# Conditioning dots moved beside wider units, one engine per portion of u, and a new order for the first norm in a streaming-encoder block

## The chip, the core and the metric

The kernel runs on one core of a Trainium2 chip. The core has a matrix engine (TensorE, in the profile PE for matmuls and PEld for the loads of their stationary operand), three engines for elementwise work (VectorE = DVE, ScalarE = ACT, GpSimd = POOL), and a queue that issues most DMAs (SyncE = SP). Each engine works through its own instructions in program order and waits for others by semaphores. The metric is the device time of one execution in microseconds (us), lower is better. The time of the kernel before is 1076.0 us, the median of three runs.

## The reference

One block works on a sequence of 512 frames with 1024 channels. All parameters are float32. With `D = 1024`, `F = 2816`:

```python
mod = (silu(c) @ w_ada + b_ada).reshape(B, 3, 3, D)      # 9 vectors of 1024 values
h = rms_norm(x, g_ffn1) * (1 + mod[:, 0, 1]) + mod[:, 0, 0]
x = x + 0.5 * mod[:, 0, 2] * swiglu(h, w_ffn1_in, w_ffn1_out)

h = rms_norm(x, g_mix) * (1 + mod[:, 1, 1]) + mod[:, 1, 0]
u_pool, u_ssm, gl_pool, gl_ssm = split(h @ w_in)         # 512, 512, 1024, 1024 channels
y_pool = multiscale_pool(u_pool, ...) @ w_pool_up
y_ssm = s5_mixer(u_ssm, ...) @ w_ssm_up                  # complex diagonal scan over time, GELU, GLU
merged = sigmoid(gl_pool) * y_pool + sigmoid(gl_ssm) * y_ssm
x = x + mod[:, 1, 2] * (merged @ w_out)

h = rms_norm(x, g_ffn2) * (1 + mod[:, 2, 1]) + mod[:, 2, 0]
x = x + 0.5 * mod[:, 2, 2] * swiglu(h, w_ffn2_in, w_ffn2_out)
return rms_norm(x, g_final)
```

`rms_norm` divides by the root of the mean of squares over the 1024 channels; `swiglu` is `(silu(h @ A) * (h @ B)) @ w_out`, with `A` and `B` of 2816 columns each. The conditioning vector `c` needs a product with a matrix of 1024 x 9216 (`w_ada`).

## The kernel before

**Layout.** Channels lie on the 128 partitions and time runs along the free dimension: `X` holds the residual stream as 8 tiles of 128 channels by 512 frames. Each float32 product is made of three matmuls of reduced-precision halves (`mm3`, lines 258 to 261): a tile of weights or activations is split into a rounded part (`hi`, made by ScalarE) and a rest (`lo`, made by VectorE), and `hi*hi`, `hi*lo` and `lo*hi` are added up in one PSUM bank.

**Units.** The program is a list of units (class `Unit`, line 46). A unit has a source of weights in HBM, a number of weight columns (at most 1024 by 128 rows), a function `mm` that issues matmuls, and optional functions `pre` and `post` around it. A unit of 1024 columns in the first feed-forward part has 24 matmuls of 512 columns, one of 640 has 15, one of 768 has 18. Units without weights (`pe_unit`) hold other work of the mixer. The loop at the end (line 1370) goes through them: `pre`, then `prefetch` (which splits the weights of a unit two ahead, and issues the DMA of one further ahead, by a plan worked out in lines 1262 to 1286), then `mm`, then `post`, then the side work of that index. Raw weights have three buffers, split ones three. The order within every engine is the program's order; nothing is rescheduled.

**Parts.** (1) The start: `c` is loaded, `silu` applied and broadcast to all partitions by two matmuls into `C`; `X` is loaded tile by tile; squares of `X` are made by ScalarE and added up by VectorE in two sums (`ACC` and `odd`, `sq_acc`, line 179); four matmuls with a column of ones turn the sum into one value for each frame (`norm_sum`); ScalarE takes the root, VectorE the reciprocal `rc`, and `norm_rows` spreads it over the partitions by matmuls with the identity `IDN`. `keep_warm` issues dummy matmuls on TensorE, as many as `WARM` tells at four places. (2) Eight units of `group6` make the first seven column groups of the feed-forward part while `h` of block `k` is being made (`make_h1`: VectorE's product `X * GS * r` at line 218 and ScalarE's rounded copy; `make_h2`: VectorE's rest at line 249). (3) The rest of the first feed-forward part goes in blocks of hidden tiles (`BLOCKS`): for every block first the units of 1024 columns that make gated hidden tiles, then eight units that multiply them by the second matrix, of 128 columns for each hidden tile of the block. (4) The mixer, (5) the second feed-forward part, where pairs of hidden tiles are made by seven products in place of eight (`ffn_seven`): each pair has units of 1024 and 768 columns, and the second ones come a step later than the first. (6) The last norm.

**Conditioning.** Each of the 72 columns of `mod` is a dot of a 128 x 1024 tile of `w_ada` with `C`, one VectorE instruction (`ada_dot`, line 132) after a DMA of 512 KB. Sixteen are made in the first eight units (shift and scale of the first norm), eight beside units 10 to 17 (the first gate), and the other 48 one by one by `ada_step`, from unit 16 on, after every unit, with two buffers: a dot, then the DMA of the next tile into the buffer just freed.

**Small work.** From unit 18 on a list `fill` gives each unit of the first feed-forward part some work on the S5 parameters: ten small VectorE operations each (`some(SMALL)`), then tables made by GpSimd (`ssm_table`), then four batches of GpSimd, TensorE and VectorE work.

**The mixer's front.** `post6` takes the first results out of PSUM. `ssm_u(m, p)` copies portion `m` of the S5 input (one PSUM bank) into `U` in sixteen pieces of 32 x 128, which reorders time and channels; `pool_in` and `pool_fin` make the pooling groups; `ssm_in`, `ssm_scan` and `ssm_out` the scan, on VectorE above all. In between stand units of gate matmuls (`gp`) that keep TensorE at work.

Of the kernel before, what the change touches and what calls it, by code (L numbers as in the profile page):

```python
# [10 lines left out]
F32 = mybir.dt.float32  # L11
F32R = mybir.dt.float32r
I32 = mybir.dt.int32
AF = mybir.ActivationFunctionType
ALU = mybir.AluOpType

P = 128
T = 512
KT = 8
NF = 22  # L20
BLOCKS = ((0, 5), (5, 10), (10, 16), (16, 22))
NPAIR = 16
WINDOWS = (2, 4, 8, 16)
EPS = 1e-6
SA = 2
LA = 4
SMALL = 10
WARM = (6, 14, 2, 6)
MAGIC = 12582912.0


# [23 lines left out]
def block_kernel(ctx, tc, a, out):  # L55
    nc = tc.nc
# [48 lines left out]
    def ev(dt=F32):  # L105
        return evp.tile([P, T], dt, tag="ev", name="ev")
# [72 lines left out]
    def sq_acc(k, eng, cs=ALL, odd=None):  # L179
        acc = odd if odd is not None and k % 2 else ACC  # L180
        if k == 0 or odd is not None and k == 1:
            S.activation(out=acc[:, cs], in_=X[:, k, cs], func=AF.Square)
        else:
            sq = ev()
            S.activation(out=sq[:, cs], in_=X[:, k, cs], func=AF.Square)  # L185
            eng.tensor_tensor(out=acc[:, cs], in0=acc[:, cs], in1=sq[:, cs], op=ALU.add)  # L186
# [4 lines left out]

    def norm_sum(pc, cs=ALL, more=()):

        b0, b1 = cs.start // P, cs.stop // P
        terms = [ACC] + list(more)
        for n, x in enumerate(terms):
            for b in range(b0, b1):
                E.matmul(pc[:, b:b + 1], x[:, b * P:(b + 1) * P], ONE[:, 0:1], start=n == 0 and b == b0,
                         stop=n == len(terms) - 1, skip_group_check=True)
        sd = smp.tile([P, 4], F32, tag="sd", name="sd")  # L200
        S.activation(out=sd[:, b0:b1], in_=pc[:, b0:b1], func=AF.Sqrt, bias=EPSC, scale=1.0 / 1024.0)
        rc = smp.tile([P, 4], F32, tag="rc", name="rc")
        V.reciprocal(out=rc[:, b0:b1], in_=sd[:, b0:b1])
        return rc
# [10 lines left out]
    def make_h1(s, k, part):  # L215
        r, cs = part
        t = ev()
        V.scalar_tensor_tensor(  # L218
            out=t[:, cs], in0=X[:, k, cs], scalar=GS[:, s * 8 + k:s * 8 + k + 1], in1=r[:, cs],
            op0=ALU.mult, op1=ALU.mult,  # L220
        )
        S.activation(out=HH[:, k, cs], in_=t[:, cs], func=AF.Identity, bias=shift_col(s, k))  # L222
        if s == 2:
            S.activation(out=HF[k % 4][:, cs], in_=t[:, cs], func=AF.Identity, bias=shift_col(s, k))
            made[k] = made.get(k, 0) + cs.stop - cs.start
        return t
# [222 lines left out]
    def ffn_seven(s, w6, win, wout, wend):  # L449
# [175 lines left out]
        def out_units(f0, f1, ds=range(KT), lastb=False):  # L625
            units.extend([out_unit([d], f0, f1, wout[d, :, f0 * P:f1 * P], [], lastb=lastb) for d in ds])
# [10 lines left out]
        for i in range(18):  # L637
            units.extend(seq[i][0])
            if i:
                units.extend(seq[i - 1][1])  # L640
            if i in (6, 12):
                out_units(i - 2, i + 4)
        units.extend(seq[17][1])
        hold = []
        units.append(out_unit(range(2), 16, 20, wend[:, 0:1024], hold, True, False))
# [77 lines left out]
    def tt_(o, x, y, op):  # L723
        vq.tensor_tensor(out=o, in0=x, in1=y, op=op)
# [272 lines left out]
    def ssm_u(m, p):  # L997
        for b in range(4):
            for t in range(4):
                o, i = U[0][32 * t:32 * t + 32, 4 * m + b, :], p[32 * b:32 * b + 32, t * P:(t + 1) * P]  # L1000
                if t % 2:
                    V.tensor_copy(out=o, in_=i)  # L1002
                else:
                    S.copy(out=o, in_=i)
# [108 lines left out]
    def mixer():  # L1113
# [95 lines left out]
        units.extend([u_unit(0), pf[3], u_unit(1), pf[2], si[0], gp[0], pf[0], sc[0], gp[1], pf[1], si[1], gp[2], sc[1], gp[3], pw_unit()])  # L1209
        units.extend([si[2], gp[4], sc[2], up[0], gp[5], si[3], up[1], sc[3], gp[6], up[2], so[0], gp[7], up[3]])  # L1210
        units.extend([so[1], gs[0], so[2], so[3]])
        units.extend(gs[1:7])
        units.extend([glu_unit(j) for j in range(4)])
        units.append(gs[7])
# [11 lines left out]
    def ada_first(n):  # L1226
        if spots:
            t = spots.pop(0)
            nc.sync.dma_start(out=t, in_=a["w_ada"][n])
            ada_tiles[n] = t  # L1230
        else:
            ada_load(n)

    def h_and_dots(k):
        t = make_h1(0, k, r0)
        if k < KT - 1:
            ada_dot(8 + k + 1)
            make_gs(0, k + 1, k + 2)
        make_h2(0, k, t, r0)
        if k < KT - 1:  # L1240
            ada_dot(k + 1)

    def pre0(k):
        if k < 3:
            ada_pair(k + 5)
        if k == 0:
            h_and_dots(0)
        if k < KT - 1:
            h_and_dots(k + 1)

    ffn(0, a["w_f1_6"], a["w_f1_in"], a["w_f1_out"], pre0)
    n_ffn1 = len(units)
    mixer()
    ffn_seven(2, a["w_f2_6"], a["w_f2_in"], a["w_f2_out"], a["w_f2_end"])

    raws, ws, due = {}, {}, []
# [7 lines left out]
    for j, u in enumerate(wu):  # L1264
        if u.kind == 2:
            t = wu.index(u.twin)
            split_at[j] = seconds[-4] + 1 if len(seconds) >= 4 else t - 1
            load_at[t] = load_at.get(t)
            seconds.append(j)
            continue  # L1270
        split_at[j] = max(walls[-3] + 1, j - 4) if len(walls) >= 3 else 0
        if j < KT:
            split_at[j] = j - 1
        walls.append(j)
        if u.kind == 1:
            jobs.append(j)
        else:
            back = split_at[raws_of[-3]] if len(raws_of) >= 3 else -9
            load_at[j] = max(split_at[j] - (3 if seconds else 2), back) if j > 3 else -1
            raws_of.append(j)  # L1280
# [7 lines left out]
    def load(j):  # L1288
        if j < len(wunits):
            u = units[wunits[j]]  # L1290
            if u.load:
                u.load()
                return
            t = rawp.tile([P, 1024], F32, tag="raw", name="raw")
            nc.sync.dma_start(out=t[:, 0:u.cols], in_=u.src)
            raws[j] = t

    def split(j):
        if j < len(wunits):
            u = units[wunits[j]]  # L1300
            if u.split:
                ws[j] = u.split()
                return
            t = raws.pop(j)[:, 0:u.cols]
            hi = wp.tile([P, 1024], F32R, tag="wh", name="wh")
            lo = wp.tile([P, 1024], F32R, tag="wl", name="wl")
            S.copy(out=hi[:, 0:u.cols], in_=t)  # L1307
            eng = G if u.pool_lo else V
            eng.tensor_tensor(out=lo[:, 0:u.cols], in0=t, in1=hi[:, 0:u.cols].bitcast(F32), op=ALU.subtract)  # L1309
            ws[j] = (hi, lo)  # L1310

    def prefetch():
        while due:
# [6 lines left out]
    def ada_pair(k):  # L1320
        ada_first(8 + k)
        ada_first(k)

    nc.sync.dma_start(out=C0, in_=a["c"].unsqueeze(0))
    for k in range(KT):
        nc.sync.dma_start(out=X[:, k, :], in_=a["x"][:, k, :])
    nc.sync.dma_start(out=COL[:, 0:120], in_=a["cols"])
    ada_first(8)
    load(0)
    ada_first(0)  # L1330
    nc.sync.dma_start(out=IDN, in_=a["ident"])
    for k in (1, 2):
        load(k)
        ada_pair(k)
# [4 lines left out]
    def keep_warm(n):  # L1339

        for _ in range(n):
            E.matmul(warm[:, 0:P], ONE, ONE, start=True, stop=True)
# [4 lines left out]
    pcs = [ps(), ps()]  # L1347
    for h in range(2):
        E.matmul(pcs[h], ONE[0:1, :], C0[:, h * T:(h + 1) * T], start=True, stop=True)
    odd = ev()  # L1350
    for d in range(KT):
        sq_acc(d, V, odd=odd)
    for h in range(2):
        S.copy(out=C[:, h * T:(h + 1) * T], in_=pcs[h])
    tt_(ACC, ACC, odd, AD)
    keep_warm(WARM[1])
    pc, r0 = ps(), ps()
    ada_dot(8)
    make_gs(0, 0, 1)
    rc = norm_sum(pc)  # L1360
    ada_dot(0)
    split(0)
    keep_warm(WARM[2])
    norm_rows(r0, rc)
    r0 = (r0, ALL)
    keep_warm(WARM[3])
    ada_pair(3)
    load(3)
    ada_pair(4)
    for i, u in enumerate(units):  # L1370
        if u.pre:
            u.pre()
        w = (None, None)
        if u.src is not None:
            j = order[i]
            due.append(j)
            w = ws.pop(j)
            if not (u.late or u.hold):
                prefetch()
        u.mm(*w)  # L1380
        if u.late:
            prefetch()
        if u.post:
            u.post()
        if 8 <= i < 16:
            nc.sync.dma_start(out=again[i - 8], in_=a["w_ada"][i + 8])
            ada_tiles[i + 8] = again[i - 8]
        if 10 <= i < 18:
            ada_dot(i + 6)
            half_gate(0, i - 10, i - 9)  # L1390
        if i >= 16:
            ada_step()
        if i >= 18 and i < n_ffn1 and fill:
            f = fill.pop(0)
            if f:
                f()
        if i == n_ffn1 - 1:
            assert not fill, len(fill)
# [90 lines left out]
```

## Time and profile before

| | us |
|---|---|
| median of three runs | 1076.0 (1075.83 to 1077.24) |
| the profiled execution | 1076.93 |
| its span, first to last instruction | 1074.9 |
| TensorE busy | 1036.9 |
| VectorE busy | 732.7 |
| ScalarE busy | 384.7 |
| GpSimd busy | 357.3 |
| mean granted TensorE clock | 0.987 |

The span is what the trace covers; around it lie another 2.0 us of the execution. A row of the timeline has the start in us, the duration, the engine, the line, the operation, the tiles (out<-in), the shapes, the number of instructions put together, and in brackets the idle time of the engine before it with what ended it. In rows of a stretch the busy time of each engine stands with its count of instructions, then the clock that TensorE was granted, the busy share of the DMA engines and GB/s. Matmuls are pipelined: their durations overlap, so the pace is read from starts or from counts. A float32 matmul that is not split shows as two records. In the list of waits a row has the waiting engine and what it writes, what it waited for, the total, the number of times and the longest.

### The profile page before, as it was taken

Reading aid. Unit: us, or ns where it says so; the run is one execution under the profiler, and the core shown is the slowest. Engines: PE = TensorE matmul, PEld = TensorE weight load, DVE = VectorE, ACT = ScalarE, POOL = GpSimd, SP = SyncE. Lnnn points to the kernel's source line nnn. Section 1 sums busy time; section 2 is a strip of 40 time slices with the busy share of each in tenths; the row PEclk is TensorE's granted clock in tenths of the full one; section 3 lists DMA queues with packets and bytes.
Section 4 is the critical chain, followed back from the end, with each engine's and each line's share of the span. In section 5 each row is a group of like instructions: output and inputs, shape, how many; then the busy total and the mean of one; then the engine's idle time right before and its main releaser. Section 6 shows DMA issues by size and latency. Waiting matters only on the chain.

```text
span 1074.9 us, 14348 instructions
## 1 busy us (share of the span) xinstructions
PE 1036.9 (96%) x5528; PEld 877.2 (82%) x5528; DVE 732.7 (68%) x1156; ACT 384.7 (36%) x565; POOL 357.3 (33%) x312
## 2 busy tenths in 40 slices
PE   8999998999999999987999999999999899999996
PEld 6788886777888889866888888887899789979986
DVE  6948788998865555668941357355899648946843
ACT  4342221222232333442334334255544224423443
POOL 1000100599552511134510000133697425714413
PEclk9999999999999999998999999999999899999998
DMA  9656554646555222411325233222333412512222
GB/s 343 233 177 213 198 180 161 225 157 211 180 197 197 85 70 70 128 30 59 118 79 157 81 96 98 79 60 88 126 120 102 154 40 81 179 56 79 84 74 79
DMA packets 46181, 138.22 MB, mean 129 GB/s; under 512 B 5137, under 2 KB 9361, under 8 KB 46114
## 3 DMA queue, kind: packets, MB, share of 16 engines
q1 hardware_dynamic: 45938, 136.73, 38.3%
q8 instruction: 43, 0.70, 0.3%
q0 software_dynamic: 176, 0.59, 0.1%
q14 instruction: 24, 0.20, 0.1%
HBM read 134.15 MB, written 3.15 MB: 128 GB/s over the span
## 4 chain that ended last, share of the span: by engine, by line
PE 79%; DVE 14%; ACT 3%; issue 2%; DMA 1%; SPq 0%; DVEq 0%; ACTq 0%
PE ps L261 18%; PE ps L259 18%; PE ps L260 18%; PE ps L490 16%; DVE wl L1309 3%; PE ps L285 2%; PE ps L284 2%; PE ps L288 2%; DVE ADA L132 2%; DVE PM L712 1%; DVE ev L710 1%; DVE U L1002 1%; DVE ev L218 1%; DMA IDN<-ident 1%; PE ps L947 1%
## 5 line engine op out<-in xcount | busy, mean ns | idle before, releaser
L1309 DVE TENSOR_TENSOR wl<-raw,wh 128x1024 fp32r<-128x1024 f32 (+4 forms) x164 | 191.2, 1169 | 92.4 <-ACT wh L1307 92.2
L261 PE MATMUL ps<-HH,wl 128*128 128x512 f32 (+1 forms) x536 | 210.7, 393 | 11.7 <-DVE wl L1309 11.7
L259 PE MATMUL ps<-HH,wh 128*128 128x512 f32 (+1 forms) x536 | 210.9, 393 | 1.5 <-ACT wh L1307 1.5
L1307 ACT CAST wh<-raw 128x1024 fp32r<-128x1024 f32 (+4 forms) x166 | 150.7, 913 | 168.2 <-PE ps L260 89.9
L260 PE MATMUL ps<-HL,wh 128*128 128x512 f32 (+1 forms) x536 | 209.5, 391 | 0.0
L261 PEld LDWEIGHTS ps<-HH,wl 128*128 128x128 f32 x536 | 101.6, 190 | 38.5 <-DVE wl L1309 15.2
L261 PE MATMUL ps<-GHA,wl 128*128 128x512 f32 (+1 forms) x308 | 118.9, 386 | 4.5 <-DVE wl L1309 4.5
L259 PE MATMUL ps<-GHA,wh 128*128 128x512 f32 (+1 forms) x308 | 119.4, 388 | 3.8 <-ACT GHA L592 3.8
L259 PEld LDWEIGHTS ps<-HH,wh 128*128 128x128 f32 x536 | 101.5, 189 | 25.2 <-ACT wh L1307 2.1
L260 PEld LDWEIGHTS ps<-HL,wh 128*128 128x128 f32 x536 | 101.7, 190 | 23.1
L260 PE MATMUL ps<-GLA,wh 128*128 128x512 f32 (+1 forms) x308 | 118.7, 385 | 1.2 <-DVE GLA L595 1.2
L651 DVE SCALAR_TENSOR_TENSOR X<-ps,MOD,X 128x512 f32<-128x512 f32 (+1 forms) x78 | 55.1, 706 | 70.1 <-PE ps L261 70.0
L186 POOL TENSOR_TENSOR ACC<-ACC,ev 128x512 f32<-128x512 f32 x15 | 19.4, 1293 | 223.2 <-ACT ev L185 223.2
L132 DVE CUSTOM_DVE_ANT_0 ADA<-ADA,C,COL 128x1024 f32<-128x1024 f32 x50 | 75.0, 1500 | 0.0
L261 PEld LDWEIGHTS ps<-GHA,wl 128*128 128x128 f32 x308 | 58.1, 188 | 18.7 <-DVE wl L1309 6.2
L259 PEld LDWEIGHTS ps<-GHA,wh 128*128 128x128 f32 x308 | 58.2, 189 | 17.1 <-ACT GHA L592 4.6
L260 PEld LDWEIGHTS ps<-GLA,wh 128*128 128x128 f32 x308 | 58.1, 189 | 14.7 <-DVE GLA L595 2.0
L285 PE MATMUL ps<-HH,wl 128*128 128x512 f32 (+1 forms) x188 | 63.8, 354 | 2.7 <-DVE wl L1309 2.5
L284 PE MATMUL ps<-HH,wh 128*128 128x512 f32 (+1 forms) x188 | 64.2, 356 | 1.2 <-ACT HH L222 1.0
L490 PE MATMUL ps<-SH,wl 128*128 128x256 f32 x216 | 60.5, 280 | 0.0
L490 PE MATMUL ps<-SH,wh 128*128 128x256 f32 x216 | 60.3, 279 | 0.0
L490 PE MATMUL ps<-SL,wh 128*128 128x256 f32 x216 | 60.2, 279 | 0.0
(255 smaller groups left out, 2119.0 us busy)
## 6 DMA issues: line engine op xcount, KB each, us to landing
ADA<-w_ada SPq DMA_DIRECT2D x50, 512.0 KB, 3.6
raw<-w_f_in SPq DMA_DIRECT2D x39, 512.0 KB, 4.4
raw<-w_f_out SPq DMA_DIRECT2D x38, 384.0 KB, 4.1
raw<-w_in SPq DMA_DIRECT2D x18, 512.0 KB, 3.7
MISC<-w_f_in SPq DMA_DIRECT2D x18, 512.0 KB, 3.5
raw<-w_f_out SPq DMA_DIRECT2D x16, 320.0 KB, 3.5
MM<-w_f_in SPq DMA_DIRECT2D x9, 512.0 KB, 3.5
ADA<-w_f_in SPq DMA_DIRECT2D x9, 512.0 KB, 3.4
```

What stands on the lines that cost most here:

```text
L132: V.tensor_tensor_reduce(out=t, in0=t, in1=C, scale=1.0, scalar=bada[:, n:n + 1], op0=ALU.mult, op1=ALU.add, accum_out=MOD[:, n:n + 1],)
L186: eng.tensor_tensor(out=acc[:, cs], in0=acc[:, cs], in1=sq[:, cs], op=ALU.add)
L259: E.matmul(pst, wh, xh, start=first, stop=False)
L260: E.matmul(pst, wh, xl, start=False, stop=False)
L261: E.matmul(pst, wl, xh, start=False, stop=last)
L284: E.matmul(pst[m][:, cs], hi[:, w], xh, start=first, stop=False)
L285: E.matmul(pst[m][:, cs], lo[:, w], xh, start=False, stop=False)
L288: E.matmul(pst[m][:, cs], hi[:, w], xl, start=False, stop=k == KT - 1)
L490: E.matmul(out_, w_[:, i, w], x_, start=first and n == 0, stop=last and n == 2, skip_group_check=True)
L651: V.scalar_tensor_tensor(out=X[:, d, cs], in0=p[:, cs], scalar=MOD[:, s * 24 + 16 + d:s * 24 + 17 + d], in1=X[:, d, cs], op0=ALU.mult, op1 ...
L1307: S.copy(out=hi[:, 0:u.cols], in_=t)
L1309: eng.tensor_tensor(out=lo[:, 0:u.cols], in0=t, in1=hi[:, 0:u.cols].bitcast(F32), op=ALU.subtract)
```

## The change

- `BLOCKS` becomes (0, 6), (6, 11), (11, 16), (16, 22): the first block has units of 768 columns in its second half, the next two units of 640.
- `ada_step` runs in the first feed-forward part only after units of 1024 columns, and in the mixer from the unit `n_gate` (after `gs[0]`, `so[2]` and `so[3]`) on.
- `ssm_u` copies a whole portion on one engine: portions 0 and 2 on ScalarE, 1 and 3 on VectorE.
- The first norm's squares are no longer added by VectorE. Each of the eight squares is summed over channels by TensorE at once, with two keep-warm matmuls ahead of each (`WARM[1]` is 2, in the loop, where 14 stood behind it). `C` is copied from PSUM by VectorE, not ScalarE. The first dots (columns 8 and 0) and the split of unit 0's weights come behind the norm; the low half of that split, the load of unit 3 and a pair of `w_ada` loads come behind the first `make_h1`. The split of unit 1 comes before the second block's `h`.
- `IDN` and the `w_ada` tile of column 0 are loaded ahead of unit 0's weights.
- In the second feed-forward part the units of the second matrix come one step of pairs later (after step 7 and 13, not 6 and 12).

```diff
-BLOCKS = ((0, 5), (5, 10), (10, 16), (16, 22))
+BLOCKS = ((0, 6), (6, 11), (11, 16), (16, 22))
-WARM = (6, 14, 2, 6)
+WARM = (6, 2, 2, 6)
...
     def norm_sum(pc, cs=ALL, more=()):
-        b0, b1 = cs.start // P, cs.stop // P
         terms = [ACC] + list(more)
         for n, x in enumerate(terms):
-            for b in range(b0, b1):
-                E.matmul(pc[:, b:b + 1], x[:, b * P:(b + 1) * P], ONE[:, 0:1], start=n == 0 and b == b0,
-                         stop=n == len(terms) - 1, skip_group_check=True)
+            squares(pc, x, cs, n == 0, n == len(terms) - 1)
+        return norm_cols(pc, cs)
+
+    def squares(pc, x, cs, first, last):
+        b0, b1 = cs.start // P, cs.stop // P
+        for b in range(b0, b1):
+            E.matmul(pc[:, b:b + 1], x[:, b * P:(b + 1) * P], ONE[:, 0:1], start=first and b == b0,
+                     stop=last, skip_group_check=True)
+
+    def norm_cols(pc, cs=ALL):
+        b0, b1 = cs.start // P, cs.stop // P
         sd = smp.tile([P, 4], F32, tag="sd", name="sd")
...
-            if i in (6, 12):
-                out_units(i - 2, i + 4)
+            if i in (7, 13):
+                out_units(i - 3, i + 3)
...
-                if t % 2:
+                if m % 2:
                     V.tensor_copy(out=o, in_=i)
                 else:
                     S.copy(out=o, in_=i)
...
         units.extend([so[1], gs[0], so[2], so[3]])
+        first_gate.append(len(units))
         units.extend(gs[1:7])
...
         t = make_h1(0, k, r0)
+        if k == 0:
+            split_lo(*w0)
+            load(3)
+            ada_pair(4)
         if k < KT - 1:
             ada_dot(8 + k + 1)
...
         if k == 0:
             h_and_dots(0)
+            split(1)
         if k < KT - 1:
             h_and_dots(k + 1)
...
         if j < KT:
-            split_at[j] = j - 1
+            split_at[j] = j - 1 if j > 1 else -1
...
+            split_lo(*split_hi(j))
+
+    def split_hi(j):
+        u = units[wunits[j]]
+        t = raws.pop(j)[:, 0:u.cols]
+        hi = wp.tile([P, 1024], F32R, tag="wh", name="wh")
+        lo = wp.tile([P, 1024], F32R, tag="wl", name="wl")
+        S.copy(out=hi[:, 0:u.cols], in_=t)
+        ws[j] = (hi, lo)
+        return j, t
+
+    def split_lo(j, t):
+        hi, lo = ws[j]
+        u = units[wunits[j]]
+        eng = G if u.pool_lo else V
+        eng.tensor_tensor(out=lo[:, 0:u.cols], in0=t, in1=hi[:, 0:u.cols].bitcast(F32), op=ALU.subtract)
...
     nc.sync.dma_start(out=COL[:, 0:120], in_=a["cols"])
+    nc.sync.dma_start(out=IDN, in_=a["ident"])
     ada_first(8)
+    ada_first(0)
     load(0)
-    ada_first(0)
-    nc.sync.dma_start(out=IDN, in_=a["ident"])
...
-    odd = ev()
-    for d in range(KT):
-        sq_acc(d, V, odd=odd)
     for h in range(2):
-        S.copy(out=C[:, h * T:(h + 1) * T], in_=pcs[h])
-    tt_(ACC, ACC, odd, AD)
-    keep_warm(WARM[1])
+        V.tensor_copy(out=C[:, h * T:(h + 1) * T], in_=pcs[h])
     pc, r0 = ps(), ps()
-    ada_dot(8)
-    make_gs(0, 0, 1)
-    rc = norm_sum(pc)
-    ada_dot(0)
-    split(0)
+    for k in range(KT):
+        sq = ev()
+        S.activation(out=sq, in_=X[:, k, :], func=AF.Square)
+        keep_warm(WARM[1])
+        squares(pc, sq, ALL, k == 0, k == KT - 1)
+    rc = norm_cols(pc)
     keep_warm(WARM[2])
     norm_rows(r0, rc)
     r0 = (r0, ALL)
     keep_warm(WARM[3])
+    ada_dot(8)
+    make_gs(0, 0, 1)
+    ada_dot(0)
+    w0 = split_hi(0)
     ada_pair(3)
-    load(3)
-    ada_pair(4)
...
-        if i >= 16:
+        if i >= 16 and (u.cols == 1024 if i < n_ffn1 else i >= n_gate):
             ada_step()
```

More of the change, by code (lines that the diff above doesn't have):

```diff
@@ L1252, in block_kernel @@
     n_ffn1 = len(units)
+    first_gate = []
     mixer()
+    n_gate = first_gate[0]
     ffn_seven(2, a["w_f2_6"], a["w_f2_in"], a["w_f2_out"], a["w_f2_end"])
@@ L1303, in split @@
                 return
[L1304 to L1310, printed above, removed]
+            split_lo(*split_hi(j))
[12 more added lines that the diff above has]
+        eng.tensor_tensor(out=lo[:, 0:u.cols], in0=t, in1=hi[:, 0:u.cols].bitcast(F32), op=ALU.subtract)
     def prefetch():
```

## The prediction

> **What bounds the kernel now.** I read the page first: the span, then the chain that ended last.
>
> ```profile
> span 1074.9 us, 14348 instructions
> ...
> PE 79%; DVE 14%; ACT 3%; issue 2%; DMA 1%; SPq 0%; DVEq 0%; ACTq 0%
> ```
>
> TensorE is the bound, so only places where it stands still, or runs at half clock, can be won. Of the chain, 14% runs over VectorE: that is where to look. TensorE's list of waits names the worst (us in total, times, longest), and busy time by stretch places the losses (length; busy us and instructions of PE, PEld, DVE, ACT, POOL; granted clock, DMA share, GB/s).
>
> ```profile
> PE ps L261 <- DVE wl L1309: 16.3, 12, 4.1
> ```
> ```profile
> 100.00:163.00 63.00, 63.00 (x272) 50.63 (x271) 48.93 (x131) 16.54 (x21) 5.41 (x4) 1.00 0.55 191
> 163.00:200.00 37.00, 31.44 (x132) 23.88 (x131) 34.56 (x104) 7.00 (x9) 9.26 (x19) 1.00 0.51 178
> 200.00:262.00 62.00, 59.40 (x253) 46.88 (x252) 58.29 (x78) 16.32 (x21) 52.58 (x37) 1.00 0.53 183
> 452.00:512.00 60.00, 50.38 (x217) 39.71 (x216) 45.63 (x95) 22.35 (x53) 25.00 (x23) 0.91 0.18 53
> 637.00:661.00 24.00, 24.00 (x105) 19.27 (x104) 20.94 (x29) 9.86 (x13) 0.00 (x0) 1.00 0.29 88
> 745.00:834.00 89.00, 89.00 (x630) 82.84 (x629) 78.64 (x96) 40.59 (x54) 62.71 (x46) 1.00 0.35 115
> 834.00:853.00 19.00, 15.26 (x80) 12.79 (x80) 15.88 (x20) 6.66 (x9) 10.73 (x9) 0.82 0.48 157
> 936.00:946.00 10.00, 8.76 (x54) 7.40 (x54) 9.45 (x14) 3.54 (x5) 6.84 (x6) 1.00 0.53 170
> ```
>
> In 100 to 163 us nothing is lost: 272 matmuls in 63 us, 0.232 us apart. At that pace the 132 of the next row need 30.6 of their 37 us (6.4 lost) and the 253 of the third 58.6 of 62 (3.4 lost): the first feed-forward part. The fourth row is the mixer's front, with 9.6 us idle and a clock of 0.91; the last two are the second feed-forward part, which the sixth shows before its first loss.
>
> **The start.** Here the change turns the order round. TensorE before, from the timeline (start, duration, count), one stretch of 1 us, a weight load, ScalarE's last squares, and VectorE:
>
> ```profile
> 3.93 3.78 PE L1349 MATMUL ps<-MISC,ONE 1*128 1x512 f32 x4
> 7.64 5.93 PE L1342 MATMUL ps<-ONE 128*128 128x128 f32 x28
> 13.43 1.05 PE L198 MATMUL ps<-ONE,ACC 128*128 128x1 f32 x8
> ```
> ```profile
> 13.00:14.00 1.00, 1.00 (x10) 0.95 (x10) 1.00 (x2) 0.00 (x0) 0.00 (x0) 1.00 1.01 414
> ```
> ```profile
> 16.94 0.29 PEld L209 LDWEIGHTS ps<-IDN,rc 128*128 128x128 f32 x1 [2.09 <-issue]
> ```
> ```profile
> 8.59 3.34 ACT L185 ACTIVATE ev<-X 128x512 f32<-128x512 f32 x5 [1.78 <-DMA X<-x]
> ```
> ```profile
> 14.81 0.18 DVE L203 RECIPROCAL rc<-sd 128x4 f32<-128x4 f32 x1
> ...
> 17.74 1.09 DVE L1309 TENSOR_TENSOR wl<-raw,wh 128x896 fp32r<-128x896 f32 x1
> 19.05 0.75 DVE L218 SCALAR_TENSOR_TENSOR ev<-X,GS,ps 128x512 f32<-128x512 f32 x1 [0.23 <-PE ps L209]
> 19.72 1.28 DVE L132 CUSTOM_DVE_ANT_0 PM<-PM,C,COL 128x1024 f32<-128x1024 f32 x1
> ...
> 26.91 1.08 DVE L1309 TENSOR_TENSOR wl<-raw,wh 128x896 fp32r<-128x896 f32 x1
> ...
> 31.84 1.09 DVE L1309 TENSOR_TENSOR wl<-raw,wh 128x896 fp32r<-128x896 f32 x1
> ```
>
> The 28 keep-warm records (two to a matmul) took 0.21 us each, yet in the microsecond from 13 ten records start: until about 12.9 us the clock was half, though no record says so, and then full. The eight records of the one-column norm sum come 0.11 apart at full clock, although each streams one column: loading 128 columns of weights sets their pace. At half clock I take twice that, 0.21; a load that nothing holds up shows 0.29 us in the half-clock stage at 16.94. Bounds: 0.11 and 0.21.
>
> Now 8 squares have 8 records of sums each and 4 of keep-warm: 96 records in TensorE's own queue behind L1349, from 7.64 us. ScalarE delivers a square each 0.67 us (five in 3.34), done by 12 us, so TensorE sets the end; VectorE's seven additions that go, and the copies of C that come to VectorE from ScalarE, lie beside that. Does the clock rise? Before it took a stretch of nothing but keep-warm to 12.9 us; L1349, back to back from 3.93, didn't raise it. Only a third of the new records stream 128 columns, so I take half clock throughout: 96 x 0.2135 = 20.5, ending at 28.1 us (before: 14.5).
>
> VectorE's dots for columns 8 and 0 now stand behind the reciprocal, which came 0.5 us after the sums (reciprocal done at 15.0 after 14.5). So 28.1 + 0.5 + 2.6 (two dots of 1.28 and a small GS) = 31.2 us for the first h, 12.2 later than 19.05. norm_rows is ready first: 0.85 of keep-warm and 8 x 0.21 end at 30.7. IDN's earlier load therefore buys nothing. The low half of unit 0, which lay in front of the first h at 17.74, comes behind it, in VectorE's unbroken row: 1.0 more. Its third split, ending at 32.9, released the steady march (one of 4.93 us per block on both engines: 26.91 to 31.84), and moving split(1) ahead changes the order only within that row. load(3) now waits for that low half, and the w_ada loads 12 and 4 queue behind it on SP, but those are wanted two marches later. **Start: +13.2 us**; with the clock rising at 12.9 as before, 25 records by then and 71 x 0.1115 after, sums end at 20.9 and it is **+5.9**.
>
> The Trainium skill (TensorE: Matmul & The Clock Gate, Part 1) says that about 3.4 us of sustained busy time releases the full clock. By it the start would be the +5.9 case or less; the trace contradicts its plain form, since from 3.93 to 12.9 us TensorE paused only briefly and stayed at half.
>
> **First feed-forward part.** The 640-column units before:
>
> ```profile
> 172.73 0.82 DVE L1309 TENSOR_TENSOR wl<-raw,wh 128x640 fp32r<-128x640 f32 x1
> ...
> 174.13 1.27 DVE L132 CUSTOM_DVE_ANT_0 ADA<-ADA,C,COL 128x1024 f32<-128x1024 f32 x1
> ...
> 178.06 0.82 DVE L1309 TENSOR_TENSOR wl<-raw,wh 128x640 fp32r<-128x640 f32 x1
> ```
>
> One round takes VectorE 5.3 us, while 15 matmuls take 3.5. Without the dot it is 4.1 at the worst, and the 112-wide table operations that make it so slide by two units into 1024-column units (24 matmuls, 5.6 us). Splits run two units ahead, so 0.6 per unit for a few units hides: **-6.4**. In 200 to 262 GpSimd's tables slow VectorE's dots and splits; the dots stay there, but VectorE arrives without a backlog. Between 0 and 3.4 I take **-2.0**. The new blocks hold as many matmuls in all.
>
> **The mixer's front.** VectorE is what TensorE waits for here (wl).
>
> ```profile
> 190.76 1.82 DVE L712 TENSOR_TENSOR PM<-PM 128x16 f32<-128x16 f32 x10
> ```
> ```profile
> 458.51 0.28 DVE L1002 COPY U<-ps 32x128 f32<-32x128 f32 x1
> 459.11 0.28 DVE L1002 COPY U<-ps 32x128 f32<-32x128 f32 x1 [0.32 <-ACT U L1004]
> ...
> 462.78 0.30 DVE L1002 COPY U<-ps 32x128 f32<-32x128 f32 x1 [0.32 <-ACT U L1004]
> 463.85 1.23 DVE L1309 TENSOR_TENSOR wl<-raw,wh 128x1024 fp32r<-128x1024 f32 x1 [0.78 <-ACT wh L1307]
> ```
>
> The copies of one portion alternate, and each waits a third of a microsecond for the other engine's: 16 copies take 4.6 us of VectorE (458.5 to 463.1), and the next cast on ScalarE stands behind them (0.78). Four portions: 18.3 us. On one engine nothing alternates; operations of one engine follow each other at 0.18 (ten in 1.82) to 0.28 us (a copy's own duration). At 0.20, portions 1 and 3 cost VectorE 3.2 each, 0 and 2 nothing: 18.3 - 6.4 + 0.8 = **-12.7**, Bounds: 0.28 gives -10.1, 0.18 gives -13.3. No more than the 9.6 us idle and the 5.4 that a clock of 0.91 loses of 60 can go. What is late next: VectorE still, which in pool_fin(2) waits for a ScalarE cast behind portion 2's copies; a few microseconds of TensorE's waits stay. Portions 0 and 2 give ScalarE eight copies more each, at up to 0.26; it was busy 22 of 60 us.
>
> **Second feed-forward part.** TensorE reached the out units' last third before the gate was stored:
>
> ```profile
> 845.94 0.79 PE L259 MATMUL ps<-GHA,wh 128*128 128x512 f32 x1 [2.76 <-ACT GHA L592]
> ```
>
> The out units now follow one step of pairs later, so 84 matmuls of 256 columns (630 in 89 us with wider ones among them: some 10 us) lie between the gate and its use, against the 2.8 us it was late. Idle 3.7 + 1.2 goes. The clock's 0.82 over 19 us is 3.4 us of full-speed work, of which some 2.9 fell on running matmuls: **-7.9**. VectorE's backlog there is about those 2.8 us, and splits run further ahead than that; a further step at its 88% (78.6 of 89) adds little. Bounds: 0 if the backlog meets TensorE, and -8.4.
>
> **The moved dots.** Of 48, 17 land between the gates and w_out, where VectorE is mostly free; not in the four w_ssm_up units (637 to 661): with four dots VectorE would want 20.9 + 5.1 of these 24 us. Between 0 and 2.1, hidden in part by the 18 matmuls that w_out does before it needs the last rows: **+0.6**. Norm sums elsewhere are only rewritten: nothing.
>
> **Sum.** 13.2 - 6.4 - 2.0 - 12.7 - 7.9 + 0.6 = -15.2. The profiled execution took 1076.9 us, span 1074.9 and 2.0 around it, 0.9 above the median of the runs (1076.0). So 1061.7 for such an execution, 1060.8 against the median: **1061 us**. A measurement of this kernel can tell about 0.2% (2 us) from no change.
>
> **The rivals.**
> - *The clock rises during the squares* (or weight loads are not slowed by half). For: TensorE's queue has no gap, and all 128 rows take part, where L1349 used one. Against: two thirds of the records stream one column. The start is then +5.9: 1061 - 7 = 1054.
> - *VectorE stays the bound where the waits were.* In the second feed-forward part its backlog, with GpSimd busy 62.7 of 89 us beside it, meets TensorE whatever the order: -7.9 falls away, 1069. For: VectorE's 88%. Against: TensorE loses nothing from 745 to 834.
> - *Slower: SP's queue.* A w_ada load waits there for the dot that frees its buffer, and the weights behind it wait too, now in the 17 units from the gates on. Loads go out two units before their split, 11.2 us.
>
> ```profile
> raw<-w_f_in SPq DMA_DIRECT2D x39, 512.0 KB, 4.4
> ```
>
> With a landing in 4.4 and the dot holding the queue some 4, about 3 us are left. It decides from there: each further microsecond costs 17 units 17 us, and 1.4 gives 1061 + 24 = 1085. For: the dot now follows posts that wait for TensorE. Against: the same pattern from 100 to 163 us lost nothing.
> - *The change doesn't do what it says.* Copies on one engine would still pay a third of a microsecond each if the wait is for the write and not for the other engine: then portions 1 and 3 cost what all did and -12.7 becomes about 0: 1074. The rows name the other engine each time; ten dependent operations at 0.18 speak against it.
>
> **Chances.** Forecast (half clock) 0.47, clock rises 0.36, VectorE's backlog 0.09, copies no quicker 0.03, slower through SP 0.05. Around the forecast, the bounds of copies, tables and second part give 1057 to 1066; around the first rival, 1050 to 1058. Leaving out the last three cases and the tails: 1049 to 1068. Faster by over 0.2% 0.92, within 0.2% 0.03, slower 0.05.
>
> **What would show it.** In the profile after: the first h of VectorE (L218's successor) at 31 us for half clock, at 24 if the clock rises; the squares' 128x1 records 0.21 or 0.11 apart; the 640-column units as dense as 100 to 163 was; U's copies 0.2 apart with no release from the other engine, and no half clock in the mixer; no wait for GHA of L592. Wrong it would be if the first h comes before 20 us, if wl still ends several waits of over 2 us in the mixer, or if raw ends any in its second half.

## The result and the profile after

The changed kernel takes 1064.1 us, the median of four runs (1061.8 to 1066.6), beside 1076.6 for the kernel before on the same chip: a ratio of 0.988, with a 95% interval of 0.985 to 0.992. The four runs lie in two pairs, 1061.8 twice and 1066.3 and 1066.6; the profiled execution is the longest of them, 1066.6 us with a span of 1064.5. Where the pairs come from is found below (experiment 5). All terms in this section are for the profiled execution, against the 1076.9 of the profiled execution before.

The page after, and TensorE's list of waits (us in total, times, longest):

```profile
span 1064.5 us, 14439 instructions
...
PE 90%; DVE 6%; ACT 3%; issue 1%; DVEq 0%; ACTq 0%
```
```profile
PE ps L268 <- DVE wl L1334: 5.1, 1, 5.1
PE ps L292 <- DVE wl L1334: 2.5, 2, 2.0
PE ps L291 <- ACT HH L229: 1.7, 4, 0.6
```

VectorE's part of the last chain fell from 14% to 6%. The wait for low halves (`wl`) that stood at 16.3 us in twelve places is 5.1 in one, and the wait for the gate `GHA` (3.8 us in two places before) is gone from the list. The same stretches as before, moved along by as much as the work in them moved:

```profile
115.00:178.00 63.00, 63.00 (x272) 50.67 (x271) 43.81 (x117) 15.13 (x19) 5.40 (x4) 1.00 0.44 154
178.00:212.00 34.00, 34.00 (x147) 26.99 (x146) 28.44 (x93) 8.08 (x12) 3.08 (x10) 1.00 0.45 148
212.00:270.00 58.00, 58.00 (x251) 46.61 (x250) 53.32 (x81) 14.91 (x19) 50.49 (x42) 1.00 0.46 159
457.00:512.00 55.00, 49.63 (x226) 40.09 (x226) 47.78 (x98) 23.97 (x55) 27.16 (x24) 0.94 0.23 71
742.00:831.00 89.00, 89.00 (x626) 82.65 (x625) 78.53 (x93) 42.85 (x56) 60.70 (x45) 1.00 0.34 110
831.00:850.00 19.00, 19.00 (x156) 18.66 (x155) 18.56 (x25) 8.59 (x12) 14.59 (x12) 1.00 0.53 177
933.00:943.00 10.00, 10.00 (x79) 9.70 (x79) 9.74 (x15) 6.92 (x10) 7.28 (x7) 1.00 0.63 216
```

- *First feed-forward part.* 147 matmuls in 34 us and 251 in 58 are 0.231 us each, the pace of the undisturbed first row. The whole loss of before, 6.4 + 3.4, is gone: **-9.8**.
- *Mixer's front.* 5.4 us idle and a clock of 0.94 (3.3 us of full speed in 55), against 9.6 and 5.4 before: **-6.3**.
- *Second feed-forward part.* No idle and full clock in the last two rows, against 3.7 + 1.2 idle and 3.4 of clock before: **-8.4**.

The start, TensorE and VectorE from the timeline (start, duration, count):

```profile
8.66 1.71 PE L202 MATMUL ps<-ONE,ev 128*128 128x1 f32 x8
10.23 1.20 PE L1366 MATMUL ps<-ONE 128*128 128x128 f32 x4
...
26.58 1.71 PE L202 MATMUL ps<-ONE,ev 128*128 128x1 f32 x8
...
46.32 0.61 PE L292 MATMUL ps<-HH,wl 128*128 128x512 f32 x1 [2.05 <-DVE wl L1334]
46.73 0.63 PE L291 MATMUL ps<-HH,wh 128*128 128x512 f32 x1
47.15 0.63 PE L292 MATMUL ps<-HH,wl 128*128 128x512 f32 x1
```
```profile
28.62 0.18 DVE L210 RECIPROCAL rc<-sd 128x4 f32<-128x4 f32 x1 [20.18 <-ACT sd L208]
...
31.39 0.74 DVE L225 SCALAR_TENSOR_TENSOR ev<-X,GS,ps 128x512 f32<-128x512 f32 x1
...
45.18 1.09 DVE L1334 TENSOR_TENSOR wl<-raw,wh 128x896 fp32r<-128x896 f32 x1
```

A square's twelve records take 2.56 us (8.66 to 11.22, and seven such steps lead to 26.58), 0.213 a record: half clock from the first square to the last. The reciprocal comes at 28.6, the first `h` (now L225) at 31.39, and the third low half at 45.18, where it stood at 31.84: **+13.3**. Behind it something stands that the prediction did not have. The matmuls after the wait that ends at 46.32 start 0.42 apart instead of 0.23: one 3.4 us stage of half clock, **+1.7**.

13.3 + 1.7 - 9.8 - 6.3 - 8.4 = -9.5; the profiled executions differ by -10.3. The 0.8 left over isn't assigned by the stretches; undoing the copies alone gives a somewhat larger term for the mixer (experiment 6).

### The profile page after: what moved, and what is told of

Read it like the earlier page. It is cut to its first block, busy times and chain, and to the rows that moved or that the text cites. A ratio compares the mean times of both kernels' runs of the same rounds, so it can differ in the third digit from the quotient of the medians.

```text
span 1064.5 us, 14439 instructions
## 1 busy us (share of the span) xinstructions
PE 1045.0 (98%) x5588; PEld 890.6 (84%) x5588; DVE 730.2 (69%) x1151; ACT 383.7 (36%) x563; POOL 352.2 (33%) x312
## 4 chain that ended last, share of the span: by engine, by line
PE 90%; DVE 6%; ACT 3%; issue 1%; DVEq 0%; ACTq 0%
PE ps L266 21%; PE ps L268 20%; PE ps L267 20%; PE ps L497 17%; PE ps L292 2%; PE ps L291 2%; PE ps L295 2%; PE ps L202 1%; DVE wl L1334 1%; PE ps L1366 1%; DVE U L1009 1%; DVE ev L225 1%; PE ps L954 1%; PE ps L1056 1%; ACT U L1011 1%
## 5 line engine op out<-in xcount | busy, mean ns | idle before, releaser
L1334 DVE TENSOR_TENSOR wl<-raw,wh 128x1024 fp32r<-128x1024 f32 (+4 forms) x164 | 194.2, 1188 | 79.7 <-ACT wh L1326 79.1
L267 PEld LDWEIGHTS ps<-HL,wh 128*128 128x128 f32 x536 | 101.1, 189 | 23.4 <-DVE HL L717 0.7
L268 PEld LDWEIGHTS ps<-GHA,wl 128*128 128x128 f32 x308 | 57.8, 188 | 13.3 <-DVE wl L1334 0.6
L267 PEld LDWEIGHTS ps<-GLA,wh 128*128 128x128 f32 x308 | 57.8, 188 | 12.7 <-DVE GLA L272 0.3
```

Source lines behind the costliest of these rows:

```text
L267: E.matmul(pst, wh, xl, start=False, stop=False)
L268: E.matmul(pst, wl, xh, start=False, stop=last)
```

## Experiments

The kernel before took 1076.3 to 1076.6 us (medians) beside these experiments. A kernel's time below is the median of its runs, with the range; experiments 4 and 5 have one run for each kernel.

### 1. The old start back

The squares are added by VectorE, `WARM` is (6, 14, 2, 6), and the first loads, dots and splits stand in the order of before; all else is as after.

```diff
-WARM = (6, 2, 2, 6)
+WARM = (6, 14, 2, 6)
...
-        squares(pc, sq, ALL, k == 0, k == KT - 1)
+        sq_acc(d, V, odd=odd)
...
-    nc.sync.dma_start(out=IDN, in_=a["ident"])
     ada_first(8)
-    ada_first(0)
     load(0)
+    ada_first(0)
+    nc.sync.dma_start(out=IDN, in_=a["ident"])
```

> The changed kernel with the start of before (squares added by VectorE, dots and the split of unit 0 ahead of the norm, the old order of loads, WARM as before); everything else as changed. Theory: the new start costs what the trace shows, the third low half ending at 46.3 us in place of 32.9 (13.3) and some 1.7 of half clock just behind it, and nothing later gives it back: 1064 - 15 = 1049 (1047 to 1052). Rival: VectorE is late for other reasons further on, so that a part of the 15 is absorbed: 1055 to 1062.

Measured: 1050.7 (1049.8 to 1051.3), 0.976 of before (0.9745 to 0.9774). VectorE's row in its timeline:

```profile
18.40 0.75 DVE L225 SCALAR_TENSOR_TENSOR ev<-X,GS,ps 128x512 f32<-128x512 f32 x1
```

The start costs 13.4 us between the medians (11.2 against the lower pair of after, 15.8 against the upper), and nothing later absorbs it. Without it the change is worth 25.6 us, about twice what it gives with it.

### 2. The new start alone

The kernel before with only the start of after.

```diff
-WARM = (6, 14, 2, 6)
+WARM = (6, 2, 2, 6)
...
+        squares(pc, sq, ALL, k == 0, k == KT - 1)
```

> The kernel before with the new start alone. Theory: 13 to 15 us slower, 1076 + 14 = 1090 (1088 to 1092), first h at 31.4 us. Rival: waits of the old kernel absorb it, since TensorE stands still there anyway: 1078 to 1084.

Measured: 1089.8 (runs 1086.9, 1087.5, 1092.1, 1092.9), 1.012 of before (1.010 to 1.015): 13.5 slower. Its waits of TensorE show that the other losses of before are still there, the wait for the gate longer than before (6.3 us against 3.8):

```profile
PE ps L268 <- DVE wl L1331: 16.7, 12, 4.3
PE ps L266 <- ACT GHA L599: 6.3, 2, 3.8
```

Experiments 1 and 2 give the same from both sides, 13.4 and 13.5 us, so as far as these medians tell the start adds to the rest and doesn't interact with it.

### 3. No keep-warm between the squares

After with the sixteen keep-warm matmuls between the squares taken out.

```diff
-WARM = (6, 2, 2, 6)
+WARM = (6, 0, 2, 6)
```

> The changed kernel with no keep-warm matmul between the squares (WARM[1] = 0). Theory: the clock is half throughout the sums with them or without, so the 32 records of 0.2135 us were only in the way: sums end at 7.65 + 64 x 0.2135 = 21.3 us, first h at 24.6, 6.8 us less: 1057. Rival: the keep-warm matmuls hold the clock for what follows, and without them the first units run at half clock: some 2 to 4 of the 6.8 come back, 1060.

Measured: 1058.9 (1058.0 to 1059.6), between the theory's 1057 and the rival's 1060. From its timeline, TensorE:

```profile
7.65 13.81 PE L202 MATMUL ps<-ONE,ev 128*128 128x1 f32 x64
...
39.48 0.50 PE L292 MATMUL ps<-HH,wl 128*128 128x512 f32 x1 [2.05 <-DVE wl L1334]
39.82 0.39 PE L291 MATMUL ps<-HH,wh 128*128 128x512 f32 x1
40.05 0.39 PE L292 MATMUL ps<-HH,wl 128*128 128x512 f32 x1
```

64 records of a one-column product, nothing else between them, take 13.8 us, 0.216 each. The 32 keep-warm records of after had cost 6.8 (46.32 against 39.48) and kept nothing warm: with them and without them the clock is half. (The runs of after that got a full stage at their start are only 2.9 above.) The stage of half clock behind the wait is missing here, too, though the wait is as long. The sums alone still leave this kernel 8.2 us behind experiment 1.

### 4. More keep-warm: first, or eight before each square

```diff
-        keep_warm(WARM[1])
+        keep_warm(14 if k == 0 else 0)
```
```diff
-WARM = (6, 2, 2, 6)
+WARM = (6, 8, 2, 6)
```

> The changed kernel with 14 keep-warm matmuls ahead of the first square and none between the others. Theory: 28 records back to back raise the clock at 13 us as before, but one-column sums do not hold it: it falls to half a stage of 3.4 us later, so about 31 records at 0.11 us and the remaining 33 at 0.21: sums end at 23.5 us, first h at 27, 4.5 less than 31.4. Rival: sums hold the clock, all 64 at 0.11: sums end at 20.1, first h at 23.4.

> The changed kernel with eight keep-warm matmuls ahead of each square in place of two: two thirds of the records stream 128 columns. Theory: the clock rises only after a stage filled almost wholly by streaming, so it stays half: 192 records of 0.2135 us end the sums at 48.6 us, first h at 51.9, 20.5 us slower than the changed kernel. Rival: two thirds suffice, the clock rises by 14 us, records 0.11 apart from there: sums end near 31, first h at 34.

One run of each: 1062.4 with fourteen in front of the first square, 1069.9 with eight before each. TensorE of the first and of the second:

```profile
7.64 5.49 PE L1366 MATMUL ps<-ONE 128*128 128x128 f32 x28
12.97 11.36 PE L202 MATMUL ps<-ONE,ev 128*128 128x1 f32 x64
```
```profile
7.64 3.78 PE L1366 MATMUL ps<-ONE 128*128 128x128 f32 x16
11.22 1.71 PE L202 MATMUL ps<-ONE,ev 128*128 128x1 f32 x8
12.78 3.66 PE L1366 MATMUL ps<-ONE 128*128 128x128 f32 x16
16.28 0.95 PE L202 MATMUL ps<-ONE,ev 128*128 128x1 f32 x8
17.09 2.03 PE L1366 MATMUL ps<-ONE 128*128 128x128 f32 x16
```

With fourteen in front, 64 records in 11.36 us are 2.4 faster than in experiment 3: one stage of 3.4 us at full clock (12.1 to 15.5 us), then half again. The first `h` came at 27.4, where the theory had 27 and the rival 23.4. With eight before each square the rival was right in kind and the theory wrong: from 16.28 on, eight sums take 0.95 us in place of 1.71, and it stays so. The clock rose later than the rival had it, at 16.2 us and not 14, and the first `h` came at 36.4, where the rival had 34 and the theory 51.9. So the clock can be held through the squares, but the keep-warm matmuls that hold it take longer (2.03 per square) than they save (0.76).

### 5. After once more

> The changed kernel once more, for its trace: its four runs lie in two groups, 1061.8 and 1066.5, and the only trace is of the upper one, where the clock falls to half from 46.6 to 50.0 us, just behind the start. Theory: the groups differ in where the clock's stages of 3.4 us fall after the start; a run of 1062 has no half clock between 34 and 60 us, one of 1066 has it. Rival: the groups differ later, in the mixer.

One run: 1061.7, beside the lower pair. Its timeline on TensorE, and then one stretch by windows (the clock is the third number from the end):

```profile
3.94 2.06 PE L1373 MATMUL ps<-MISC,ONE 1*128 1x512 f32 x4
5.93 0.71 PE L1366 MATMUL ps<-ONE 128*128 128x128 f32 x4
6.48 0.95 PE L202 MATMUL ps<-ONE,ev 128*128 128x1 f32 x8
...
8.06 1.71 PE L202 MATMUL ps<-ONE,ev 128*128 128x1 f32 x8
...
43.15 0.50 PE L292 MATMUL ps<-HH,wl 128*128 128x512 f32 x1 [2.03 <-DVE wl L1334]
43.48 0.39 PE L291 MATMUL ps<-HH,wh 128*128 128x512 f32 x1
```
```profile
10.50:14.00 3.50, 3.50 (x19) 3.50 (x18) 0.00 (x0) 0.63 (x1) 0.00 (x0) 0.50 1.03 419
```

Same program, another clock. Here the four broadcast matmuls take 2.06 us (3.78 in the longer run, as before the change): one stage at full clock right at the start, from 4.1 to 7.5 us, then half. The wait that ended at 46.32 ends at 43.15, 3.2 earlier, and the matmuls behind it start 0.23 apart, so the 1.7 falls away as well. 3.2 + 1.7 = 4.9 us is the distance of the two executions (1061.7 against 1066.6). Only these two have a trace, but the mean clock on record for the other runs goes with it: 0.983 for the lower pair, as here, and 0.992 for the upper. Experiment 2 shows two pairs as well, 5.3 us apart. What the theory expected of this run, no half clock between 34 and 60 us, held; that it also has a full stage in front of the squares was not expected.

In these traces the clock changes on a grid of 3.413 us that runs on its own: in both executions the stages are that long or multiples of it, but they begin elsewhere against the program. Laid over the timelines, the stage from 4.1 us came out full here after one with keep-warm matmuls in 84% of it (1.08 to 3.94 of 0.72 to 4.13). In the longer run the same matmuls fill 51% of their stage (2.19 to 5.61, counted back from the first recorded one at 32.91), and the next was half. Likewise behind the idle 2 us: in the longer run they lie whole within one stage (43.15 to 46.56), which is then busy for 1.4 of 3.4 us, and the next is half; here the grid cuts them in two, at 41.68, and nothing follows; in experiment 3 the stage is busy for 1.6 us (35.80 to 39.21), and the next stays full.

### 6. The copies of u as before

```diff
-                if m % 2:
+                if t % 2:
```

> The changed kernel with the copies of u alternating between VectorE and ScalarE as before. Theory, from the traces: copies on one engine come 0.30 us apart (16 in 4.79), so VectorE won only the two portions that ScalarE took, and waits 2.5 us behind one of these; from the end of the first eight units to the low half of the fifth gate unit 57.6 us became 50.5: 7.1 slower, 1071. Rival, the forecast's term: 12.7 slower, 1077. Rival: the wait that remains is set by the half clock, and the copies matter little: 1064 to 1067.

Measured: 1072.7 (two runs at 1069.4 and 1070.2, three from 1072.7 to 1073.9). Pair against pair it is 8.0 slower than after in the lower and 6.9 in the upper (means: 1069.8 against 1061.8, 1073.4 against 1066.5). The view of the tile `U` says what ended the idle time before its instructions (us, times):

```profile
its engine sat idle before it (us, times) until:
  DVE U L1009: 18.1, 28
  ACT U L1011: 9.1, 28
```

28 waits of 0.65 us and 28 of 0.33, each for the other engine's copy. In after that list is empty, and the copies stand together:

```profile
458.21 4.31 ACT L1011 COPY U<-ps 32x128 f32<-32x128 f32 x16
...
465.26 4.79 DVE L1009 COPY U<-ps 32x128 f32<-32x128 f32 x16
...
472.76 4.27 ACT L1011 COPY U<-ps 32x128 f32<-32x128 f32 x16
...
482.11 4.79 DVE L1009 COPY U<-ps 32x128 f32<-32x128 f32 x16
```

The change does what it says, but a portion costs VectorE 4.79 us, 0.30 a copy, and not the 3.2 of the prediction.

### 7. All four portions on ScalarE

On the kernel of experiment 1:

```diff
-                if m % 2:
-                    V.tensor_copy(out=o, in_=i)
-                else:
-                    S.copy(out=o, in_=i)
+                S.copy(out=o, in_=i)
```

> The kernel of e1 with all four portions of u copied by ScalarE. Theory: copies cost 0.27 to 0.30 us each on any engine, and what counts is how many stand in VectorE's row: 9.6 us of them go, VectorE waits some 2 us more for casts behind them, so the one wait of 5.3 us that is left in the mixer's front and its half clock nearly go: 1050.7 - 6 = 1044.7. Rival: ScalarE becomes the bound (17 us of copies ahead of the casts that the splits need), no gain: 1050 to 1053.

Measured: 1046.0 (1045.7 to 1047.1), 4.7 faster than experiment 1. Its mixer (windows) and its waits of TensorE:

```profile
443.00:498.00 55.00, 52.38 (x242) 42.51 (x241) 45.68 (x75) 34.34 (x88) 30.40 (x26) 0.97 0.21 67
```
```profile
PE ps L268 <- DVE wl L1326: 2.6, 2, 2.2
```

TensorE is idle for 2.6 us of the 55 (5.8 in experiment 1, where the clock was 0.94), with a clock of 0.97. ScalarE has the room: 34.3 us busy of 55. This is, with experiment 9, the fastest version, 0.972 of before (0.971 to 0.974).

### 8. The dots of before, and the out units of before

Each on the kernel of experiment 1.

```diff
-BLOCKS = ((0, 6), (6, 11), (11, 16), (16, 22))
+BLOCKS = ((0, 5), (5, 10), (10, 16), (16, 22))
...
-        if i >= 16 and (u.cols == 1024 if i < n_ffn1 else i >= n_gate):
+        if i >= 16:
```
```diff
-            if i in (7, 13):
-                out_units(i - 3, i + 3)
+            if i in (6, 12):
+                out_units(i - 2, i + 4)
```

> The kernel of e1 (changed, with the start of before) with a conditioning dot after every unit and the old blocks. Theory: the dots beside 640-column units were the whole of the first feed-forward part's loss; the gaps between matmuls from 163 to 262 us came to 10.2 us before and to 0.24 after, so 10 slower than e1's 1050.7: 1060.7. Rival, the forecast's terms (the tables of GpSimd keep their share): 8.4 slower, 1059. Rival: VectorE's later lateness takes up most of it, under 5 slower, 1055.

> The kernel of e1 with the units of the second matrix in the second feed-forward part where they were (after steps 6 and 12). Theory: the two waits for a gate and the half clock behind the first come back, by the gaps between matmuls 8.5 us: 1059. Forecast's term 7.9: 1058.6. Rival: only the idle time counts, 5: 1055.7.

Measured: 1060.3 (1060.0 to 1060.5) for the dots, 9.6 slower than experiment 1; 1059.1 (1058.2 to 1059.8) for the out units, 8.4 slower. The first undoes the dots and the blocks together, so it doesn't tell what each is worth. The waits that come back, of the first and of the second kernel:

```profile
PE ps L268 <- DVE wl L1329: 13.3, 9, 5.1
```
```profile
PE ps L266 <- ACT GHA L599: 4.0, 2, 2.9
```

### 9. The sums on VectorE with the new loads and order

Experiment 7, with `IDN` and the tile of column 0 loaded early as in after, the low half of unit 0 (with the load of unit 3) behind the first `h`, and the split of unit 1 ahead of the second. The dots stay where they were before. The diff shows the loads only.

```diff
     nc.sync.dma_start(out=COL[:, 0:120], in_=a["cols"])
+    nc.sync.dma_start(out=IDN, in_=a["ident"])
     ada_first(8)
+    ada_first(0)
     load(0)
-    ada_first(0)
-    nc.sync.dma_start(out=IDN, in_=a["ident"])
```

> The kernel of e7 with the squares added by VectorE as before, but the identity and the tile of column 0 loaded ahead of unit 0's weights, the low half of unit 0 behind the first h and the split of unit 1 ahead of the second, as the change has them. Theory: the first h then waits for neither load and comes at 17 us in place of 18.4, of which 1.0 is given back by the low half in VectorE's row: 0 to 1 less than e7. Rival: the later landing of unit 0's weights delays it: 0 to 1 more.

Measured: 1046.2 (1044.8 to 1046.3), no difference from experiment 7 that can be measured. VectorE in experiment 7, then here:

```profile
18.34 0.74 DVE L225 SCALAR_TENSOR_TENSOR ev<-X,GS,ps 128x512 f32<-128x512 f32 x1
...
31.12 1.09 DVE L1326 TENSOR_TENSOR wl<-raw,wh 128x896 fp32r<-128x896 f32 x1
```
```profile
16.31 0.75 DVE L225 SCALAR_TENSOR_TENSOR ev<-X,GS,ps 128x512 f32<-128x512 f32 x1
...
30.33 1.08 DVE L1331 TENSOR_TENSOR wl<-raw,wh 128x896 fp32r<-128x896 f32 x1
```

Its first `h` came 2 us earlier, but the low half that starts the steady march only 0.8. So the new loads and splits neither cost nor bring anything that these runs can tell, and the price of the new start lies in what is left of it: the sums on TensorE, with the keep-warm matmuls among them, and the two dots behind them. The dots weren't moved alone; in the trace of after they end at 31.39, 0.3 us behind the matmuls that spread the norm (29.14 and 1.92 long), so they can account for little of it.

## Why the prediction was right, point by point

The forecast was 1061, and its case, half clock through the squares, is the one that ran; only the first square of the shorter execution had the full clock. The two pairs of runs lie at 1061.8 and 1066.5, both inside the range of 1049 to 1068; the upper one lies at the edge of the 1057 to 1066 given for the forecast's own case.

- **The start**, +13.2: measured +13.3 in the profiled execution, with the first `h` at 31.39 (31.2 predicted) and 0.213 us a record. The reason fits: at half clock a one-column record takes 0.21 us, as the keep-warm records of 128 columns do, and still does with none of these in between (experiment 3), and the loads of 128 columns leave no gap (PEld, the second busy time in the windows row of experiment 5, has 3.50 of 3.50 us). No run changed the width of the load, so that it is the load stays argued. What was missing is the phase. The shorter execution has +10.1 (13.3 less 3.2), the longer one another 1.7 in the stage behind the third low half.
- **The rival "the clock rises"**, +5.9: it gave a time of 1054, and no run of the changed kernel was below 1061.7. Its weak point was the row from which it was read: before, the clock rose after a stretch of keep-warm alone, and the change leaves a third of that. Experiment 4 shows that the mix can be made dense enough, at a loss. The Trainium skill (TensorE: Matmul & The Clock Gate, Part 1) calls the window of activity free-running, 3413 ns long, and the cold start of one kernel different from run to run. The traces agree: stages of 3.413 us, and 4.9 us between two executions of this program. The prediction had used its other sentence, on 3.4 us of sustained work, and not this one.
- **First feed-forward part**, -6.4 - 2.0: measured -9.8. The first term was right, the second lay at the far end of its bounds, -3.4: with no backlog, VectorE takes GpSimd's tables, dots and splits without TensorE noticing (58.0 of 58 us busy in that stretch). Experiment 8 gives 9.6 for the dots and the blocks together; which of the two matters more stays open.
- **The mixer's front**, -12.7, is the term that was mis-sized: -6.3 by the stretches, -6.9 to -8.0 by undoing it. It failed at "At 0.20, portions 1 and 3 cost VectorE 3.2 each". The row behind that 0.20 showed operations on 16 elements per partition, which last about 0.18 themselves; a copy of 128 lasts 0.28, and copies of one engine follow at their own duration and a little, 0.30 measured. That lies outside the bounds of 0.18 to 0.28, too. 18.3 - 2 x 4.79 leaves 8.7. The rest went where the prediction had named a wait and not priced it, the cast behind portion 2's copies:

```profile
477.71 0.69 DVE L272 TENSOR_TENSOR GLA<-ev,GHA 128x512 fp32r<-128x512 f32 x1 [2.52 <-ACT GHA L271]
```

  8.7 - 2.5 + 0.8 for the cast that no longer waits is 7.0. The low half that TensorE wants then comes 5.1 us late (the first row of the waits after), and the clock falls to half from 493.7 to 500.5 us. So two of the signs that the prediction had named for this part, copies 0.2 apart and no half clock in the mixer, did not show.
- **Second feed-forward part**, -7.9: measured -8.4, the bound; experiment 8 gives 8.4. The rival in which VectorE's backlog meets TensorE there did not come: 18.6 of 19 us busy, and TensorE lost nothing.
- **The moved dots**, +0.6, and **the rival through SP's queue**: neither shows. In 635 to 659 us, the units of `w_ssm_up`, TensorE is busy for 24.00 of 24 us with the dots there. The only waits for `raw` are two of ScalarE, 7.8 us in total, at 203 and 287 us in the first feed-forward part, where TensorE stood still for neither; none lies in the mixer.

The near hit of the total is partly luck. The mixer brought some 5 to 6 us less than forecast, the two feed-forward parts 2 more and the start cost up to 1.8 more, or 3 less; only in the lower pair do these nearly cancel.

## What to carry to other kernels

A one-column matmul here cost as much as one of 128 columns at the same clock, because, as far as these traces show, each needs its own load of 128 columns: eight squares summed on TensorE cost 64 loads where one sum costs 8, and adding up on an idle VectorE first was 8.2 us cheaper without keep-warm between the sums (experiment 3 against 1) and 13.4 with it. Take the pace of a run of small operations from one of the same shape, and never below that operation's own duration. When work changes engine to stop two engines from waiting for each other, look which of them is late already; here all of it belonged on ScalarE (experiment 7, 4.7 us).

## What the runs showed of the hardware

- The clock column of the profile is no witness before the first recorded stage. For after it shows 1.00 up to 32.9 us, while matmuls run at half pace; the other execution of the same program has records there, and they say 0.50 (the windows row of experiment 5). The pace of the matmuls tells it in both.
- TensorE shown busy without a gap doesn't bring the full clock: it was 3.50 of 3.50 us busy in every window from 10.5 to 28 us of after. What went with the clock in these runs was the share of wide matmuls: squares with 40% of their time in keep-warm (1.0 of 2.56 us) stayed half, 70% (1.87 of 2.68 us, experiment 4) stayed full. By single stages of experiment 4's second kernel it is closer: 9.39 to 12.80 us, at half clock with 54% keep-warm, was followed by half, and 16.21 to 19.62, at full clock with 57%, by full. Where the limit lies, and whether a full clock needs less to stay than a half one to rise, these runs don't settle.
- A pause of 2 us cost another 1.7 us or nothing, and this went with where the 3.413 us grid cut it (three executions in experiment 5; in experiment 4's first kernel the stage of 39.39 to 42.80 us was busy for 1.4 us, and the next was half).
